# Trailing sums of the pooling moved to VectorE, a fifth first block, more last blocks by token halves, and the chain of 1/rms placed among them

## The chip, the cores and the metric

The kernel runs on one core of a Trainium2 chip, in one launch. The core has five engines with an instruction queue each: TensorE (PE: matmuls; the loads of its weights are listed as PEld), VectorE (DVE), ScalarE (ACT), GpSimd (POOL) and SyncE (SP, which here only starts transfers). The metric is the device time of one execution in microseconds (us). Lower is better.

## The reference

Two layers, each a token mixer and a feed-forward network (FFN) on 512 tokens of 1024 numbers, with a root-mean-square norm ahead of and behind each of the four parts. Cut to what the change touches:

```python
def rms_norm(x, w):
    return x * lax.rsqrt(jnp.mean(x * x, axis=-1, keepdims=True) + RMS_EPS) * w

def multiscale_pool(u, w_lin, scale):      # POOL_WINDOWS = (2, 4, 8, 16), 4 groups of 128
    cs = jnp.cumsum(groups, axis=1)
    for gi, win in enumerate(POOL_WINDOWS):
        pooled.append((c - prev) / cnt)    # trailing mean over win tokens
    mixed = jnp.stack(pooled, axis=2) - groups
    y = jnp.einsum('bsgc,gcd->bsgd', mixed, w_lin)
    return y * scale

def reference(x, ...):
    for l in range(DEPTH):                 # DEPTH = 2
        m = hybrid_mixer(rms_norm(x, mix_pre_norm[l]), ...)
        x = x + rms_norm(m, mix_post_norm[l])
        h = rms_norm(x, ffn_pre_norm[l])
        x = x + rms_norm(swiglu(h, ...), ffn_post_norm[l])
```

The mixer multiplies its input by one wide matrix whose columns feed a gated DeltaNet (q, k, v with a short convolution, two gates a and b), the pooling above, a retention and three gates; the three results go through a branch matrix each, are gated and added, and go through `w_out`. The FFN is `(silu(h @ w_gate) * (h @ w_up)) @ w_down` with 2816 hidden columns.

## The kernel before

**Layout.** The hidden dimension lies on the 128 partitions, in 8 tiles `k`; the 512 tokens lie along the free axis. A block is 128 output columns for all tokens: 8 products over `k` into one PSUM bank. Each product is three matmuls (`mm3`, L223 to L225), because weights and operands are split into a high and a low part: hh·wh, hl·wh, hh·wl. So a block is 24 matmuls of 128x512, or, if it is done by token halves, 48 of 128x256. The weights come by SyncE's queue into three buffers `raw`, and are split half a block at a time by ACT (`wh`, L233) and DVE (`wl`, L234) into `WB` = 8 buffers each.

**Order.** Generators are advanced by hand (`some(gen, n)`, `tasks`, `fill`) and so write the instructions in an order in which PE always has a next matmul; the splitting of weights runs ahead under a raised priority, and the scheduler of the framework then sets each engine's order. Engines execute in order and wait for each other by semaphores.

**Hand-over** (`hand_over`) is the passage from the mixer to the FFN and back; there are three inside the kernel, and a last one that writes the result. The last blocks of a stage (`LAST_OUT`, `LAST_DOWN` of them) are done by token halves h0 and h1. When a half is complete, `mean_square` sums its squares over the partitions with matmuls against ones (L268); DVE then takes 1/rms in eleven small operations in a chain (`rsv` L270, then L244 to L260, the last writes `rsy`), and `spread_new` copies it over the partitions with matmuls (L276). `step(h, ps, k)` then makes the new x of one tile k and half h: `pt` (L329) and `xt` (L330) on DVE, its high part `hh` (L229, ACT) and low part `hl` (L230, DVE), its square (ACT) and the running sum of squares (POOL, L290). The first blocks of the next stage do not wait for its own 1/rms: `group_step` multiplies three of them side by side (PSUM tiles `cx`), and the factor `rb` is applied to the results.

**Start of a mixer.** The first four blocks are the pooling's inputs. Behind `rb`, DVE writes them as `ku` (L1130); `pooled` makes the trailing sums `ft` by doubling, ten per layer, on POOL (L966); DVE then makes the mixed tile with one wide operation (L970) and two of 16 columns (L974, L977); and `pool_map` multiplies it on PE (L983), whose result ACT and DVE split into `oh` and `ol`. Among them stand the convolution of key block 0 (L608 to L629) and the two gates a, b of all heads: `abw` (L510, L511) is multiplied on PE (L516, 16 matmuls), the result scaled on DVE (`cv`, L519) and transposed on PE (L522).

## Time and profile before

| what | value |
|---|---|
| median of 3 runs | 1876.48 us (1874.4 to 1877.54) |
| profiled execution, its own time | 1876.93 us |
| its span in the trace | 1875.1 us |
| mean granted clock of TensorE | 0.989 of full speed |
| busy: PE, DVE, ACT, POOL | 1819.5, 1045.0, 711.9, 394.7 us |

The span is what the trace covers, from the first to the last recorded work; the profiled execution's time is 1.83 us more, and lies 0.45 us above the median. PE is busy for 97% of the span. [...]

### The profile page before, as it was taken

What the parts mean: (1) busy time and instruction counts of PE and PEld (TensorE: products, weight loads), DVE (VectorE), ACT (ScalarE), POOL (GpSimd) and SP (SyncE); (2) the same over time, 40 slices, a digit from 0 to 9 for tenths busy, and PEclk for the clock granted to TensorE, in tenths of its full rate; (3) what the DMA queues carried; (4) which work ended last, traced back from release to release, by engine and by line L of the source; (5) the groups of instructions that cost most, each with busy time, mean ns of one, the idle gap of its engine ahead of it and who ended that gap; (6) DMA issues with size and microseconds to landing.
All of it is one profiled execution on the core that took longest, in us unless ns stands there. A gap on an engine that the chain in (4) does not pass through costs nothing.

```text
span 1875.1 us, 24737 instructions
## 1 busy us (share of the span) xinstructions
PE 1819.5 (97%) x9286; PEld 1531.2 (82%) x9286; DVE 1045.0 (56%) x1973; ACT 711.9 (38%) x1259; POOL 394.7 (21%) x364
## 2 busy tenths in 40 slices
PE   8899999999999999999979999999999999999997
PEld 6677888888898888888867878888888888888887
DVE  7668667664438442344486786666644564324433
ACT  4553333343344333333345533334333443333332
POOL 4130211012223220222250302110121332102212
PEclk9899999999999999999989999999999999999998
DMA  5223212124225323223232222222243252333321
GB/s 194 70 80 93 74 60 71 60 87 146 91 71 188 96 96 102 92 100 95 76 118 93 80 83 62 69 72 67 90 135 101 70 188 92 102 93 98 101 90 46
DMA packets 65415, 177.70 MB, mean 95 GB/s; under 512 B 15376, under 2 KB 18448, under 8 KB 65296
## 3 DMA queue, kind: packets, MB, share of 16 engines
q1 hardware_dynamic: 54016, 172.78, 28.4%
q10 hardware_dynamic: 11280, 3.34, 0.8%
q8 instruction: 73, 1.20, 0.3%
q14 instruction: 46, 0.38, 0.1%
HBM read 167.18 MB, written 8.39 MB: 94 GB/s over the span
## 4 chain that ended last, share of the span: by engine, by line
PE 84%; DVE 9%; ACT 2%; issue 1%; POOL 1%; ACTq 1%; DMA 1%; SPq 0%; DVEq 0%; POOLq 0%
PE pp L223 24%; PE pp L225 24%; PE pp L224 24%; DVE ct L618 2%; DVE wl L234 2%; POOL ft L966 1%; DVE hl L230 1%; ACTq L787 1%; PE cx L820 1%; PE cx L913 1%; PE cx L903 1%; DVE xt L330 1%; PE cx L805 1%; PE fx L499 1%; ACT wh L233 1%
## 5 line engine op out<-in xcount | busy, mean ns | idle before, releaser
L233 ACT ACTIVATE wh<-raw 128x512 fp32r<-128x512 f32 x584 | 364.8, 629 | 718.4 <-PE pp L224 626.3
L223 PE MATMUL pp<-hh,wh 128*128 128x512 f32 x1568 | 623.7, 398 | 0.0
L225 PE MATMUL pp<-hh,wl 128*128 128x512 f32 x1568 | 614.1, 392 | 0.0
L224 PE MATMUL pp<-hl,wh 128*128 128x512 f32 x1568 | 612.5, 391 | 0.0
L234 DVE TENSOR_TENSOR wl<-raw,wh 128x512 fp32r<-128x512 f32 x584 | 418.0, 719 | 316.2 <-ACT wh L233 300.6
L225 PEld LDWEIGHTS pp<-hh,wl 128*128 128x128 f32 x1568 | 294.9, 188 | 63.9 <-issue 1.2
L223 PEld LDWEIGHTS pp<-hh,wh 128*128 128x128 f32 x1568 | 295.1, 188 | 61.2 <-issue 2.3
L224 PEld LDWEIGHTS pp<-hl,wh 128*128 128x128 f32 x1568 | 295.3, 188 | 59.4 <-issue 0.5
L223 PE MATMUL pp<-ah,wh 128*128 128x512 f32 (+1 forms) x418 | 149.1, 357 | 0.0
L225 PE MATMUL pp<-ah,wl 128*128 128x512 f32 (+1 forms) x418 | 148.6, 356 | 0.0
L224 PE MATMUL pp<-al,wh 128*128 128x512 f32 (+1 forms) x418 | 148.5, 355 | 0.0
L1255 POOL TENSOR_TENSOR gs<-gt,sg 128x512 f32<-128x512 f32 x44 | 56.7, 1288 | 314.3 <-ACT sg L1253 314.3
L1260 POOL TENSOR_TENSOR a<-gs,ut 128x512 f32<-128x512 f32 x44 | 70.2, 1594 | 136.1 <-DVE ut L1258 135.8
L290 POOL TENSOR_TENSOR sqa<-sqa,sq 128x256 f32<-128x256 f32 (+1 forms) x69 | 62.6, 907 | 127.9 <-ACT sq L283 108.6
L225 PEld LDWEIGHTS pp<-ah,wl 128*128 128x128 f32 x418 | 79.0, 189 | 11.3
L223 PEld LDWEIGHTS pp<-ah,wh 128*128 128x128 f32 x418 | 78.9, 189 | 11.3
L224 PEld LDWEIGHTS pp<-al,wh 128*128 128x128 f32 x418 | 79.0, 189 | 11.3
L234 DVE TENSOR_TENSOR al<-a,ah 128x512 fp32r<-128x512 f32 x44 | 31.3, 711 | 77.7 <-ACT ah L233 77.5
L1005 POOL TENSOR_TENSOR y<-y,ft 128x512 f32<-128x512 f32 x16 | 27.2, 1702 | 184.8 <-DVE ft L1004 95.3
L233 ACT ACTIVATE ah<-a 128x512 fp32r<-128x512 f32 x44 | 27.8, 632 | 89.2 <-POOL a L1260 89.2
L1258 DVE TENSOR_TENSOR ut<-pp,rb 128x512 f32<-128x512 f32 x42 | 29.0, 690 | 58.7 <-PE pp L225 58.7
L223 PE MATMUL pp<-yh,wh 128*128 128x256 f32 (+1 forms) x192 | 61.4, 320 | 0.0
(306 smaller groups left out, 2441.6 us busy)
## 6 DMA issues: line engine op xcount, KB each, us to landing
raw<-in_wi_dram SPq DMA_DIRECT2D x117, 512.0 KB
raw<-in_wgu_dram SPq DMA_DIRECT2D x88, 512.0 KB
raw<-in_wd_dram SPq DMA_DIRECT2D x44, 512.0 KB
raw<-in_wbr_dram SPq DMA_DIRECT2D x24, 512.0 KB
raw<-in_wo_dram SPq DMA_DIRECT2D x16, 512.0 KB
xd<-xt SPq DMA_DIRECT2D x24, 256.0 KB
xt<-xd SPq DMA_DIRECT2D x24, 256.0 KB
xt<-in_x_dram SPq DMA_DIRECT2D x16, 256.0 KB
```

What stands on the lines that cost most here:

```text
L223: T.matmul(ps, lhsT=w[0], rhs=m[0], start=start, stop=False)
L224: T.matmul(ps, lhsT=w[0], rhs=m[1], start=False, stop=False)
L225: T.matmul(ps, lhsT=w[1], rhs=m[0], start=False, stop=stop)
L230: V.scalar_tensor_tensor(out=lo, in0=src, scalar=scalar, in1=hi.bitcast(F32), op0=ALU.mult, op1=ALU.subtract)
L233: A.activation(out=hi, in_=src, func=AF.Copy)
L234: V.tensor_tensor(out=lo, in0=src, in1=hi.bitcast(F32), op=ALU.subtract)
L290: G.tensor_tensor(out=t, in0=acc[0], in1=acc[1], op=ALU.add)
L618: V.scalar_tensor_tensor(out=a2, in0=u[:, j : j + S], scalar=tap(j), in1=a, op0=ALU.mult, op1=ALU.add)
L1005: G.tensor_tensor(out=ys[n], in0=ys[n], in1=t, op=ALU.add)
L1255: G.tensor_tensor(out=gs, in0=gt, in1=sg, op=ALU.mult)
L1258: V.tensor_tensor(out=ut, in0=up, in1=rb, op=ALU.mult)
L1260: G.tensor_tensor(out=a, in0=gs, in1=ut, op=ALU.mult)
```

## The change

It moves the ten trailing sums of each layer from POOL to DVE (same tiles, same sizes; L966 becomes L975). A stage now starts with five blocks: three side by side, a fourth also by token halves (`alone`), and a fifth for all tokens (`last_block`); for the mixer the fifth is convolution block 0 of the keys, for the FFN the gate of column block 2, which were done a little later before. Six blocks of `w_out` and four of `w_down` go by token halves, rather than four and three; homes for the split weights of the last two weight tiles (`beside`) make room for them. The places of the steps and of the two chains of 1/rms change: all eight `step(0, …)` now stand among the last blocks of the old stage, the chain of h1 starts behind tile 4 of the h0 group, its `spread_new` stands before `alone(h0)`. In the mixer, key block 1 comes ahead of the first two pool maps, and the two products of the rotary tables with `rb` (`rotations`) are written later; on POOL they stand first all the same.

```diff
-LAST_OUT = 4
-LAST_DOWN = 3
+LAST_OUT = 6
+LAST_DOWN = 4
...
-        def __init__(self, src, cut=False):
+        def __init__(self, src, cut=False, home=None):
+            self.home = home or (lambda a: wpool.tile([P, S], F32R, tag=a, bufs=WB, name=nm(a)))
...
-                wh = wpool.tile([P, S], F32R, tag="wh", bufs=WB, name=nm("wh"))
-                wl = wpool.tile([P, S], F32R, tag="wl", bufs=WB, name=nm("wl"))
+                wh, wl = self.home("wh"), self.home("wl")
...
         r = mean_square(accs[0])
-        some(p1, 4)
+        with tc.issue_after(nc.cur_bb.bb.instructions[-1]):
+            some(p1, 5)
         ps0 = spread_new(r)
...
-        for k in range(3):
+        for k in range(KT):
             step(0, ps0, k)
             some(p1, 2)
         rest(p1)
-        step(0, ps0, 3)
         ws, pss = [weights(src) for src in srcs[:3]], [psum_c() for _ in range(3)]
+        w4th, ps4 = weights(srcs[3]), psum_p()
+
+        def alone(sl):
+            for k in range(KT):
+                group_step([w4th], [ps4], hs, sl, k)
+                yield
+
         for k in range(KT):
             group_step(ws, pss, hs, h0, k)
-            if k == 0:
+            if k == 4:
                 r = mean_square(accs[1])
-            if k == 4:
-                ps1 = spread_new(r)
-            if k < 4:
-                step(0, ps0, k + 4)
-            elif k >= 5:
-                step(1, ps1, k - 5)
+        f = alone(h0)
+        ps1 = spread_new(r)
+        for k in range(3):
+            step(1, ps1, k)
+            some(f, 3)
+        r = mean_square(pre[0])
         for k in range(KT):
             group_step(ws, pss, hs, h1, k)
-            if k == 1:
-                r = mean_square(pre[0])
-            if k == 4:
-                A.activation(out=rb[:, h0], in_=spread_new(r), func=AF.Copy)
             if k + 3 < KT:
                 step(1, ps1, k + 3)
-        f = fourth_block(srcs[3], hs, pss)
+            if k == 6:
+                A.activation(out=rb[:, h0], in_=spread_new(r), func=AF.Copy)
+        rest(alone(h1))
+        f = last_block(srcs[4], hs, pss)
+        pss.append(ps4)
...
-        return vec[:, l, V_PRE1 : V_PRE1 + KT], [wi[l, B_PU + g] for g in range(4)]
+        return vec[:, l, V_PRE1 : V_PRE1 + KT], [wi[l, B_PU + g] for g in range(4)] + [wi[l, B_K]]
...
-        return vec[:, l, V_PRE2 : V_PRE2 + KT], [wgu[l, 0, 0], wgu[l, 0, 1], wgu[l, 1, 0], wgu[l, 1, 1]]
+        return vec[:, l, V_PRE2 : V_PRE2 + KT], [wgu[l, f // 2, f % 2] for f in range(5)]
...
                 t = ft()
-                G.tensor_tensor(out=t[:, first:], in0=src[:, first:], in1=src[:, first - d : S + pad - d], op=ALU.add)
+                V.tensor_tensor(out=t[:, first:], in0=src[:, first:], in1=src[:, first - d : S + pad - d], op=ALU.add)
...
-            G.tensor_tensor(out=t, in0=t, in1=rb, op=ALU.mult)
+
+        def rotations():
+            for t in (crb, srb):
+                G.tensor_tensor(out=t, in0=t, in1=rb, op=ALU.mult)
+            yield
...
-        tasks = convs("k", 0) + [pool_map(0), pool_map(1)] + convs("k", 1)
+        tasks = convs("k", 0) + convs("k", 1) + [pool_map(0), pool_map(1)]
...
-        tasks += convs("v", 0) + p(7)
+        tasks += [rotations()] + convs("v", 0) + p(7)
...
-                    held[n] = weights(wo[l, n])
+                    held[n] = weights(wo[l, n], home=beside() if n >= KT - 2 else None)
...
-                            held[i // 8] = weights(wd[l, half, i // 8])
+                            last = half == 1 and i // 8 >= KT * HALF // 8 - 2
+                            held[i // 8] = weights(wd[l, half, i // 8], home=beside if last else None)
```

The first of three places is VectorE's queue at the start of the first mixer, up to `cv`, the scaled gates a and b. The names: `ft` are trailing sums, or in L608 and L616 the convolution's input; `kr`, `qr`, `vc`, `mask` are the four mixed tiles of the pooling, `pc` their first 16 columns; `wl` are low parts of weights, `ct` steps of the convolution. Before:

```order
L234 TENSOR_TENSOR wl_702<-raw_682,wh_701 128x512 [waits PE_49,Activation_49]
L974 TENSOR_TENSOR pc_388<-ft_384,kc 128x16 [waits DVE_49]
L977 TENSOR_TENSOR vc_386<-pc_388,ku_349 128x16 [waits DVE_49]
L970 SCALAR_TENSOR_TENSOR mask_399<-ft_397,ku_349 128x496 [waits Pool_49]
L974 TENSOR_TENSOR pc_401<-ft_397,kc 128x16 [waits DVE_49]
L608 TENSOR_TENSOR ft_444<-pp_411,rb_127 128x512 [waits PE_49]
L977 TENSOR_TENSOR mask_399<-pc_401,ku_349 128x16 [waits DVE_49]
L234 TENSOR_TENSOR wl_736<-raw_732,wh_735 128x512 [waits DMAHW2_49,Activation_49]
L618 SCALAR_TENSOR_TENSOR ct_449<-ft_444,vec,ct_447 128x512 [waits Activation_49]
L618 SCALAR_TENSOR_TENSOR ct_451<-ft_444,vec,ct_449 128x512 [waits DVE_49]
L618 SCALAR_TENSOR_TENSOR ct_453<-ft_444,vec,ct_451 128x512 [waits DVE_49]
L519 TENSOR_TENSOR cv_482<-fx_459,rb_127 16x512 [waits PE_49]
```

and after:

```order
L979 SCALAR_TENSOR_TENSOR vc_419<-ft_417,ku_384 128x496 [waits DVE_49]
L983 TENSOR_TENSOR pc_421<-ft_417,kc 128x16
L975 TENSOR_TENSOR ft_426<-ft_424 128x525 [waits DVE_49]
L986 TENSOR_TENSOR vc_419<-pc_421,ku_384 128x16 [waits DVE_49]
L234 TENSOR_TENSOR wl_700<-raw_680,wh_699 128x512 [waits PE_49,Activation_49]
L975 TENSOR_TENSOR ft_428<-ft_426 128x521 [waits DVE_49]
L234 TENSOR_TENSOR wl_734<-raw_730,wh_733 128x512 [waits DMAHW2_49,PE_49,Activation_49]
L975 TENSOR_TENSOR ft_430<-ft_428 128x513 [waits DVE_49]
L616 TENSOR_TENSOR ft_442<-pp_341,rb_127 128x512
L979 SCALAR_TENSOR_TENSOR mask_432<-ft_430,ku_384 128x496 [waits DVE_49]
L983 TENSOR_TENSOR pc_434<-ft_430,kc 128x16
L527 TENSOR_TENSOR cv_524<-fx_486,rb_127 16x512 [waits PE_49]
```

The sums, which POOL did beside this queue, now stand in it one by one, and `cv` has moved ahead of the convolution's three steps.

The second place is TensorE's queue a little further on in the same mixer: the end of the 16 matmuls of the gates (`abw`), the transposes of `cv`, and the first pool map (`sw` holds the map's weights). Before:

```order
L516 MATMUL fx_459<-hh_125,abw_348 128x512
L516 MATMUL fx_459<-hl_126,abw_348 128x512
L983 MATMUL fx_476<-kr_366,sw_351 128x512 [waits DMAHW4_49,DVE_49,Activation_49]
L223 MATMUL pp_510<-hh_111,wh_511 128x512
L224 MATMUL pp_510<-hl_112,wh_511 128x512
L225 MATMUL pp_510<-hh_111,wl_512 128x512
L522 MATMUL fx_484<-kc,cv_482 128x8 [waits DVE_49]
L522 MATMUL fx_484<-kc,cv_482 128x8 x3
L223 MATMUL pp_510<-hh_113,wh_511 128x512
```

and after:

```order
L524 MATMUL fx_486<-hh_125,abw_383 128x512
L524 MATMUL fx_486<-hl_126,abw_383 128x512
L223 MATMUL pp_459<-hh_123,wh_476 128x512
L224 MATMUL pp_459<-hl_124,wh_476 128x512
L225 MATMUL pp_459<-hh_123,wl_477 128x512
L223 MATMUL pp_459<-hh_125,wh_476 128x512
L224 MATMUL pp_459<-hl_126,wh_476 128x512
L225 MATMUL pp_459<-hh_125,wl_477 128x512
L530 MATMUL fx_526<-kc,cv_524 128x8 [waits DVE_49,Activation_49]
L530 MATMUL fx_526<-kc,cv_524 128x8 x3
L992 MATMUL fx_531<-kr_399,sw_386 128x512 [waits DMAHW4_49,PE_49]
L223 MATMUL pp_578<-hh_111,wh_579 128x512
```

The pool map of `kr` has moved behind the transposes, and 6 matmuls rather than 3 stand between the gates' last matmul and the transposes. What no row here shows: key block 1, 24 matmuls of the fifth block's kind, begins ahead of the gates rather than behind them.

The third place is VectorE's queue in the hand-over from the first mixer to its FFN, at the chain of 1/rms of the half h1 (`rsv` to `rsy`, 128x2 each). Before:

```order
L329 TENSOR_TENSOR pt_5229<-m_4884,fx_4991 128x256
L250 TENSOR_TENSOR rsb_5163<-rsa_5161,rsv_5155 128x2 [waits DVE_49]
L230 SCALAR_TENSOR_TENSOR hl_5005<-xt_4073,vec,hh_5004 128x256 [waits Activation_49]
L252 SCALAR_TENSOR_TENSOR rsa_5165<-rsb_5163 128x2 [waits DVE_49]
L230 SCALAR_TENSOR_TENSOR hl_5007<-xt_4076,vec,hh_5006 128x256 [waits Activation_49]
L254 SCALAR_TENSOR_TENSOR rsy_5167<-rsa_5165,rsy_5159 128x2 [waits DVE_49]
L330 SCALAR_TENSOR_TENSOR xt_4076<-pt_5229,vec,xt_4076 128x256
L256 SCALAR_TENSOR_TENSOR rsa_5169<-rsy_5167 128x2 [waits DVE_49]
L234 TENSOR_TENSOR wl_5462<-raw_5459,wh_5461 128x512 [waits DMAHW0_49]
L258 TENSOR_TENSOR rsb_5171<-rsa_5169,rsv_5155 128x2 [waits DVE_49]
L230 SCALAR_TENSOR_TENSOR hl_5009<-xt_4076,vec,hh_5008 128x256 [waits Activation_49]
L260 SCALAR_TENSOR_TENSOR rsy_5173<-rsb_5171,rsy_5167 128x2 [waits DVE_49]
```

and after:

```order
L234 TENSOR_TENSOR wl_5379<-raw_5221,wh_5378 128x512 [waits PE_49,Activation_49]
L270 TENSOR_SCALAR rsv_5298<-fx_5293 128x2 [waits PE_49]
L244 TENSOR_SCALAR rsi_5300<-rsv_5298 128x2 [waits DVE_49]
L246 TENSOR_SCALAR rsy_5302<-rsi_5300 128x2 [waits DVE_49]
L248 TENSOR_TENSOR rsa_5304<-rsy_5302 128x2 [waits DVE_49]
L250 TENSOR_TENSOR rsb_5306<-rsa_5304,rsv_5298 128x2 [waits DVE_49]
L252 SCALAR_TENSOR_TENSOR rsa_5308<-rsb_5306 128x2 [waits DVE_49]
L254 SCALAR_TENSOR_TENSOR rsy_5310<-rsa_5308,rsy_5302 128x2 [waits DVE_49]
L256 SCALAR_TENSOR_TENSOR rsa_5312<-rsy_5310 128x2 [waits DVE_49]
L258 TENSOR_TENSOR rsb_5314<-rsa_5312,rsv_5298 128x2 [waits DVE_49]
L260 SCALAR_TENSOR_TENSOR rsy_5316<-rsb_5314,rsy_5310 128x2 [waits DVE_49]
L329 TENSOR_TENSOR pt_5348<-m_4601,fx_5345 128x256 [waits PE_49]
```

Before, steps of the half h0 (`xt`, `pt`, `hl`) and a low part of weights stand between the links of the chain; now the links follow each other, and the first step of the half h1 comes behind the last.

## Rows read from the trace of the kernel before

**Rows 1.** TensorE's waits over the span: for what, us in total, times, longest

```profile
PE fx L276 <- DVE rsy L260: 10.7, 8, 2.5
PE fx L522 <- DVE cv L519: 9.4, 1, 9.4
PE fx L516 <- DVE qr L977: 8.5, 1, 8.5
```

**Rows 2.** Windows (us, busy PE, PEld, DVE, ACT, POOL, granted clock): both mixers' starts

```profile
46.00:55.00 9.00, 0.18 (x1) 0.00 (x0) 7.57 (x14) 0.75 (x2) 4.20 (x5) 0.65 0.21 58
971.00:984.00 13.00, 4.52 (x11) 3.47 (x11) 11.96 (x18) 0.91 (x2) 11.01 (x11) 0.61 0.00 0
```

**Rows 3.** TensorE's timeline at the starts: start, us, instruction, count, idle before

```profile
40.83 0.39 PE L516 MATMUL fx<-hh,abw 128*128 128x512 f32 x1
...
44.45 1.02 PE L983 MATMUL fx<-kr,sw 128*128 128x512 f32 x2
...
55.54 1.87 PE L522 MATMUL fx<-kc,cv 16*128 16x8 f32 x8 [9.36 <-DVE cv L519]
57.34 0.80 PE L223 MATMUL pp<-hh,wh 128*128 128x512 f32 x1
...
62.50 1.02 PE L983 MATMUL fx<-qr,sw 128*128 128x512 f32 x2
...
979.67 0.77 PE L516 MATMUL fx<-hh,abw 128*128 128x512 f32 x1 [8.48 <-DVE qr L977]
...
985.40 1.02 PE L983 MATMUL fx<-kr,sw 128*128 128x512 f32 x2
...
987.27 1.05 PE L522 MATMUL fx<-kc,cv 16*128 16x8 f32 x8
```

**Rows 4.** VectorE's timeline at the starts of both mixers

```profile
34.82 1.89 DVE L1130 TENSOR_TENSOR ku<-cx,rb 128x512 f32<-128x512 f32 x3 [1.77 <-ACT rb L381]
...
38.47 1.52 DVE L970 SCALAR_TENSOR_TENSOR kr<-ft,ku 128x496 f32<-128x496 f32 x1 [1.17 <-POOL ft L966]
...
50.36 0.68 DVE L970 SCALAR_TENSOR_TENSOR mask<-ft,ku 128x496 f32<-128x496 f32 x1 [1.16 <-POOL ft L607]
50.95 0.17 DVE L974 TENSOR_TENSOR pc<-ft,kc 128x16 f32<-128x16 f32 x1
...
54.81 0.67 DVE L519 TENSOR_TENSOR cv<-fx,rb 16x512 f32<-16x512 f32 x1
...
965.26 1.88 DVE L1130 TENSOR_TENSOR ku<-cx,rb 128x512 f32<-128x512 f32 x3 [0.82 <-ACT rb L455]
```

**Rows 5.** GpSimd's timeline at the first mixer's start: first and last trailing sums

```profile
37.38 2.09 POOL L966 TENSOR_TENSOR ft<-ku 128x527 f32<-128x527 f32 x2
...
46.04 4.28 POOL L966 TENSOR_TENSOR ft<-ft 128x525 f32<-128x525 f32 x3
```

**Rows 6.** Windows as in rows 2: in the first hand-over, around the second

```profile
569.00:575.00 6.00, 5.02 (x30) 5.05 (x31) 5.74 (x16) 2.81 (x8) 1.44 (x2) 0.72 0.54 188
920.00:965.00 45.00, 42.05 (x314) 39.24 (x314) 39.09 (x106) 22.27 (x52) 13.02 (x16) 1.00 0.40 133
```

**Rows 7.** Timeline of the first hand-over, and TensorE's last L276 of the kernel

```profile
563.73 0.14 DVE L270 TENSOR_SCALAR rsv<-fx 128x2 f32<-128x2 f32 x1
563.77 0.28 PE L223 MATMUL cx<-hh,wh 128*128 128x256 f32 x1
...
564.97 0.28 PE L224 MATMUL cx<-hl,wh 128*128 128x256 f32 x1
...
569.98 0.68 PE L276 MATMUL fx<-kc,rsy 128*128 128x128 f32 x4 [2.46 <-DVE rsy L260]
570.70 0.42 DVE L329 TENSOR_TENSOR pt<-m,fx 128x256 f32<-128x256 f32 x1 [0.26 <-PE fx L276]
...
584.27 0.87 DVE L230 SCALAR_TENSOR_TENSOR hl<-xt,vec,hh 128x256 fp32r<-128x256 f32 x2
...
1865.78 0.55 PE L276 MATMUL fx<-kc,rsy 128*128 128x128 f32 x1 [2.12 <-DVE rsy L260]
```

More of the change, by code (lines that the diff above doesn't have):

```diff
@@ L351, in rest, with last_block @@
             pass
-    def fourth_block(src, hs, res):
+    def last_block(src, hs, res):
         ps = psum_p()
@@ L376, in begin @@
             group_step(ws, pss, hs, WHOLE, k)
-        f = fourth_block(srcs[3], hs, pss)
+        f = last_block(srcs[3], hs, pss)
         some(f, 1)
@@ L382, in begin @@
         rest(f)
+        rest(last_block(srcs[4], hs, pss))
         return x_in, hs, rb, pss
@@ L408, in hand_over @@
                     send(h0, k // 2)
-                some(p1, 1)
+                some(p1, 2)
             rest(p1)
@@ L430, in hand_over @@
         rest(p1)
-        step(0, ps0, 3)
         ws, pss = [weights(src) for src in srcs[:3]], [psum_c() for _ in range(3)]
+        w4th, ps4 = weights(srcs[3]), psum_p()
[3 more added lines that the diff above has]
+                yield
         for k in range(KT):
             group_step(ws, pss, hs, h0, k)
-            if k == 0:
+            if k == 4:
                 r = mean_square(accs[1])
-            if k == 4:
-                ps1 = spread_new(r)
-            if k < 4:
-                step(0, ps0, k + 4)
-            elif k >= 5:
-                step(1, ps1, k - 5)
+        f = alone(h0)
[4 more added lines that the diff above has]
+        r = mean_square(pre[0])
         for k in range(KT):
             group_step(ws, pss, hs, h1, k)
-            if k == 1:
-                r = mean_square(pre[0])
-            if k == 4:
-                A.activation(out=rb[:, h0], in_=spread_new(r), func=AF.Copy)
             if k + 3 < KT:
                 step(1, ps1, k + 3)
-        f = fourth_block(srcs[3], hs, pss)
+            if k == 6:
[3 more added lines that the diff above has]
+        pss.append(ps4)
         some(f, 1)
@@ L636, in conv_one @@
         def conv_one(b, ch, key):
-            res = []
-            yield from project(wi[l, b], hs, res)
+            res = firsts[4:] if key == ("k", 0) else []
+            if not res:
+                yield from project(wi[l, b], hs, res)
             o = conv(res[0], ch, key)
@@ L1204, in mixer, with beside, home @@
             ms, acc, held = [], None, {}
+            def beside():
+                t = {a: keep.tile([P, D], F32R, tag="wq", bufs=H, name=nm(a)) for a in ("wh", "wl")}
+                n = dict(wh=0, wl=0)
+                def home(a):
+                    n[a] += 1
+                    return t[a][:, (n[a] - 1) * S : n[a] * S]
+                return home
             def out_block(n, sl, res):
                 if n not in held:
-                    held[n] = weights(wo[l, n])
+                    held[n] = weights(wo[l, n], home=beside() if n >= KT - 2 else None)
                     ms.append(keep.tile([P, S], F32, tag="y", bufs=KT, name=nm("m")))
@@ L1236, in run @@
             def run(f, i):
-                if 2 * f + i < 4:
+                if 2 * f + i < len(firsts):
                     return firsts[2 * f + i]
@@ L1266, in ffn, with beside @@
                 held = {}
+                free = iter(("gt", "sg", "gt", "sg", "gs", "ut", "gs", "ut"))
+                def beside(a):
+                    return tl(next(free), 2, dt=F32R)
                 def down(n, sl, res):
```

## The prediction

> **What bounds the kernel now.** TensorE is busy for 97% of the span, so I looked first for where it is not: its list of waits [rows 1]. Three entries stand out, and the change touches all three. One wait of 9.4 us at the transposes of `cv` (L522) and one of 8.5 us at the gates' matmuls (L516) are the starts of the two mixers; 10.7 us in eight pieces are waits of `spread_new` (L276) for the end of the chain of 1/rms, 2.1 us of them at the very end of the kernel [rows 7], which the change hardly touches. So 8.6 us lie in the three hand-overs inside the kernel.
>
> Then the windows: around the long waits the granted clock is a mix, 0.65 and 0.61 [rows 2], so each wait costs more than its length. The timeline prices that. [...] Start of the first mixer: 9.36 idle, 12 × 0.204 = 2.4 for the matmuls, and 0.8 because the transposes took 1.87 rather than 1.05 us: **12.6 us lost**. Start of the second: 8.48 idle, and the 16 matmuls behind it took 979.67 to 985.40, 5.73 rather than 3.62 us: **10.6 us lost**. In the first hand-over the longest L276 wait, 2.46 us [rows 7], is followed by a stretch of six microseconds at 0.72 [rows 6]: 0.28 of 6 us missing, halving the speed for some 3.4 us, costs about 1.5 us. I take the same for the third hand-over, of the same shape. The second has no wait so long, and its window shows 1.00 [rows 6]. Hand-overs: 8.6 + 3.0 = **11.6 us lost**.
>
> What VectorE waits for at the starts is GpSimd: "[1.17 <-POOL ft L966]" [rows 4]. The ten sums there ran from 37.38 to 50.32, 12.9 us [rows 5]. And while they run, VectorE itself is slow: the same wide operation L970 took 1.52 us beside them and 0.68 us behind them [rows 4].
>
> **Sums on VectorE.** The trace shows none. The nearest row is `ku`, a two-input operation of 128x512: three took 1.89 us, 0.60 each with a tail [rows 4]; 527 columns make 0.62. From below: not under 0.60. From above: 1.45, the distance by which the 1.52 us operations would follow each other. I take 0.62, since after the change GpSimd holds only the two rotary products in this stretch.
>
> [...]
>
> **First mixer.** Along the new order VectorE has, from 34.82 [rows 4]: four `ku` 2.4, ten sums 6.2, four wide mixing operations at 0.6 (0.68 less the overlap) 2.4, seven of 16 columns at 0.09 (50.95, next at 51.04) 0.6, three `wl` and the convolution's input at 0.6 2.4. That is 48.9, and `cv` takes 0.67: 49.6. TensorE stood at 40.83 at the gates [rows 3]; now 18 matmuls of key block 1 come first (44.9), then the gates (48.5), then 6 more (49.9). So `cv` is just ready and the 9.36 us are gone, with the low clock. `cv` also stood behind three convolution steps at 0.6 to 0.8 and no longer does; these come later, where the next to need them is many matmuls away. What becomes late next: the four pool maps, closer together now, each needing ScalarE's `oh` and VectorE's `ol` (0.7 us each by the width of `cv`) and one of two PSUM banks. I put 2.0 us for that (bounds 0 and 6): **−10.6**.
>
> **Second mixer.** From 965.26: `ku` 2.4, eight sums 5.0, three wide 1.8, six narrow 0.5 and the cast: the gates' operand at 975.2. TensorE came there at 971.19 (979.67 less 8.48) and has 22 matmuls more first: 976.2. No wait. The gates end at 979.8, `cv` at 980.9 (VectorE is free at 979.6), TensorE is there at 980.7. Behind it the new order crowds all four maps into some twenty instructions: 0.9 for the first `oh` (a map of 0.46, then 0.7), 0.4 and 0.5 for banks, 0.5 for an `ol`: with 0.2 at `cv` 2.5 us (bounds 0 and 7): **−8.1**.
>
> **Hand-overs.** Before, the chain of h1 took from 563.73 to 569.98 [rows 7], since steps stand between its links; TensorE had 24 matmuls meanwhile, and 128x256 go at 0.120 us (563.77 to 564.97 for ten), 2.9 us. After, the links follow each other: eleven operations of 0.15 to 0.2, 2.2 us with the wait for L268's result some 2.5, and 27 matmuls (3.2 us) to cover it. That holds if the eight steps of h0 are done by then: 24 operations at 0.35 to 0.40 and three `wl` are 11 us, beside 17 us of TensorE (102 matmuls of the last blocks and five tiles of h0). The h1 steps with the next chain were 14.4 us of VectorE (570.70 to 585.14); from L276 to the last `hl` TensorE has some 14 us (102 matmuls of 128x256, two L276, one L268). So that is even, and I leave 1.7 us of waits in each hand-over (bounds 0 and the present 3.9): 11.6 − 5.1 = **−6.5**. Moving a wait's start alone would bring nothing; what shortens it is the interleaved work taken out of the chain.
>
> **Halves.** 48 × 0.120 less 24 × 0.226 is 0.33 us per block. Two more blocks of `w_out` in two layers 1.3; one of `w_down` (33 products) in two layers 0.9; the fourth block in three hand-overs 1.0: **+3.1** (no cover: TensorE pays). The fifth block replaces one done later: 0. `beside` adds no instruction: 0, unless the fourth weight tile comes late (below).
>
> **Sum.** 1876.93 (the profiled execution, span 1875.1, 0.45 above the median) − 10.6 − 8.1 − 6.5 + 3.1 = **1854.8, so 1855**.
>
> **Rivals.**
> *A, the wait moves to the pool maps.* For it: all four maps within twenty instructions in the second mixer, two banks. Against: each wait is under a microsecond by the rows. At the upper bounds, 4 and 4.5 us more: 1863.5.
> *B, hand-overs give nothing.* The chain of h1 stands behind both `wl` of the fourth block's weights; there are three `raw` buffers, so this tile is fetched only after an earlier one is split. If it comes as TensorE reaches L276, the wait stays. Against: some 4 us of VectorE's work and over 10 of TensorE's lie between. 1876.9 − 18.7 + 3.1 = 1861.3.
> *C, all clean.* Half a microsecond left at each of the five places: 34.8 less 2.5, 1876.9 − 32.3 + 3.1 = 1847.7.
> *D, VectorE stays as slow as it is beside GpSimd now; slower.* If the sums and mixing operations take 1.45 and the narrow ones 1.0 us, `cv` comes 14 × 0.84 + 7 × 0.9 = 18 us later at each start; the waits stay, with the low clock behind (3.2 and 2.1): 18 + 3 − 1 each, 1854.8 + 39 = 1894. It decides (ends above 1880.2) from some 12.7 us per start, 0.75 us on each wide operation. Against: two rotary products of GpSimd cannot cover twenty operations.
> *E, no effect.* The order shows the sums in VectorE's queue, so only gains and losses that cancel make it: sums and mixing operations at about 1.25 us.
>
> **Chances.** Forecast 0.52, A 0.14, B 0.16, C 0.12, D 0.03, E 0.03. The range runs from just under C to just over A, 1846 to 1866, and holds some 0.85. A difference of 0.2% (3.75 us) is about what a measurement of this kernel can tell from none: faster 0.94, same 0.03, slower 0.03.
>
> **What would show it.** Right: no wait over 1.5 us at L530 and L524; granted clock 1.0 from 36 to 75 us and behind the second `ku`; L975 near 0.7 us, L979 0.68 and L983 0.17; waits at L276 together under 6 us, and no low clock in the hand-overs. Wrong: L975 at 1 us or more (D, E), waits at L992 or at products of `oh` over 3 us (A), an L276 wait over 2 us behind `wl` (B). The whole fails if another place, quiet now, loses what these win, above all VectorE's later backlog of convolution steps.

## The result, and the profile after

| | before | after |
|---|---|---|
| median | 1876.38 us (4 runs) | 1849.58 us (4 runs, 1848.3 to 1850.55) |
| ratio to before | | 0.9857, 95% interval 0.9844 to 0.9870 |
| profiled execution, span | 1876.93, 1875.1 us | 1850.22, 1848.4 us |
| mean granted clock | 0.989 | 0.996 |

The forecast was 1855, with a range of 1846 to 1866; the kernel became 26.8 us faster, 5 us more than forecast. TensorE's list of waits over the span (for what, us in total, times, longest), where [rows 1] stood before:

```profile
PE cx L223 <- ACT wh L233: 6.1, 1, 6.1
PE fx L276 <- DVE rsy L260: 4.0, 4, 2.1
PE fx L507 <- DVE cv L633: 3.2, 8, 0.6
PE cx L224 <- DVE hl L230: 2.7, 4, 1.8
PE cx L912 <- ACT c L914: 2.5, 1, 2.5
```

The waits of 9.4 and 8.5 us are gone (the 6.1 us at the head of the list are the kernel's very first matmul), and those at L276 fell from 10.7 to 4.0 us, 2.1 of them at the end of the kernel. The window over the first mixer's start, then two stretches in the second mixer which are told of below (columns as in [rows 2]):

```profile
36.00:75.00 39.00, 39.00 (x176) 30.65 (x175) 34.91 (x78) 20.55 (x32) 3.17 (x8) 1.00 0.21 71
970.00:973.00 3.00, 2.58 (x4) 1.44 (x5) 2.06 (x5) 1.00 (x3) 0.00 (x0) 0.59 0.55 180
1107.00:1113.00 6.00, 3.93 (x16) 3.35 (x17) 2.49 (x4) 4.13 (x8) 2.13 (x3) 0.79 0.28 90
```

TensorE is busy for all 39 us of the first, at full clock (1.00). VectorE's timeline there, the answer to [rows 4]:

```profile
37.37 1.39 DVE L975 TENSOR_TENSOR ft<-ku 128x527 f32<-128x527 f32 x2
38.68 0.66 DVE L979 SCALAR_TENSOR_TENSOR kr<-ft,ku 128x496 f32<-128x496 f32 x1
39.26 0.16 DVE L983 TENSOR_TENSOR pc<-ft,kc 128x16 f32<-128x16 f32 x1
39.35 0.69 DVE L975 TENSOR_TENSOR ft<-ft 128x525 f32<-128x525 f32 x1
39.96 0.17 DVE L986 TENSOR_TENSOR kr<-pc,ku 128x16 f32<-128x16 f32 x1
...
48.93 0.67 DVE L527 TENSOR_TENSOR cv<-fx,rb 16x512 f32<-16x512 f32 x1
```

A sum takes 0.69 us and the next operation starts 0.61 us after it; the first two, one behind the other, took 1.39. The mixing operation takes 0.66, not 1.52 us, the narrow ones 0.16, not 1.03. TensorE's timeline at the transposes shows no idle time before them:

```profile
49.81 0.39 PE L225 MATMUL pp<-hh,wl 128*128 128x512 f32 x1
50.13 1.05 PE L530 MATMUL fx<-kc,cv 16*128 16x8 f32 x8
51.11 1.13 PE L992 MATMUL fx<-kr,sw 128*128 128x512 f32 x2
```

The start of the second mixer, TensorE's timeline from the gates' transposes on:

```profile
967.56 1.03 PE L530 MATMUL fx<-kc,cv 16*128 16x8 f32 x8
968.52 1.12 PE L992 MATMUL fx<-kr,sw 128*128 128x512 f32 x2
970.42 0.72 PE L223 MATMUL pp<-oh,wh 128*128 128x512 f32 x1 [0.78 <-ACT oh L229]
970.94 1.91 PE L992 MATMUL fx<-qr,sw 128*128 128x512 f32 x2
972.64 1.68 PE L992 MATMUL fx<-vc,sw 128*128 128x512 f32 x2
973.57 0.98 PE L224 MATMUL pp<-ol,wh 128*128 128x512 f32 x1
```

Two pool maps take 1.91 and 1.68 rather than 1.02 us: behind a wait of 0.78 us the granted clock was lower (0.59 over these 3 us, above). The first hand-over, chain of h1 and its L276, then L276 of the next chain and one late `hl`, VectorE first, then TensorE, as in [rows 7]:

```profile
555.76 0.16 DVE L270 TENSOR_SCALAR rsv<-fx 128x2 f32<-128x2 f32 x1 [0.98 <-PE fx L268]
...
557.54 0.16 DVE L260 SCALAR_TENSOR_TENSOR rsy<-rsb,rsy 128x2 f32<-128x2 f32 x1
```

```profile
558.90 0.60 PE L276 MATMUL fx<-kc,rsy 128*128 128x128 f32 x4
...
569.35 0.68 PE L276 MATMUL fx<-kc,rsy 128*128 128x128 f32 x4 [0.62 <-DVE rsy L260]
573.07 0.38 PE L224 MATMUL cx<-hl,wh 128*128 128x256 f32 x1 [0.30 <-DVE hl L230]
```

The chain took 1.94 us from first to last link, where before 6.25 us passed from its first link to L276 [rows 7], and was ready 1.2 us ahead of TensorE. What is left is 0.62 and 0.30 us.

To see where the time went, I cut the spans at the same places of the program: the first L276 that makes `rb`; the first transpose of the convolved values (L499 before, L507 after); the first product of `w_out`; the first of each half of `w_down`; the last L276 that makes `rb` of the second mixer; the end of the last transfer's issue, some 3 us ahead of the end of the span. Kernels with the fifth block have 20 matmuls of 0.227 us (4.5 us) in hand-over 2 that else stand in the start of mixer 2: the 24 of the fifth block, less four, because the last L276 comes behind 22 matmuls of its block before and behind 18 after. So the sum of these two stages is a line of its own. In us, from the profiles of all kernels with the sums on either engine (a2 is the changed kernel once more; e1 to e4 are told below):

```
stage             before   after      a2      e1      e2      e3      e4
to first L276       33.1    33.2    32.9    33.0    33.3    35.6    33.5
mixer 1 start      150.8   138.6   138.6   150.9   138.6   138.3   148.0
mixer 1 rest       329.5   330.6   330.8   330.4   329.3   333.1   329.5
hand-over 1        177.4   173.7   173.7   173.7   177.3   177.3   173.7
FFN 1              179.5   179.5   179.5   179.5   179.5   179.5   179.5
hand-over 2         93.9    95.4    95.4    95.4    93.9    94.0    95.4
mixer 2 start      147.7   135.3   133.7   141.7   138.8   138.2   141.8
mixer 2 rest       329.8   333.2   333.4   330.3   330.1   330.4   329.2
hand-over 3        177.4   173.7   173.7   173.7   176.1   176.1   173.7
FFN 2              179.5   179.5   179.5   179.5   179.5   179.5   179.5
end                 73.4    72.8    73.3    73.3    72.9    72.9    72.8
h-o 2 + m 2 st.    241.6   230.7   229.1   237.1   232.7   232.2   237.2
all               1872.0  1845.5  1844.4  1861.3  1849.4  1855.0  1856.6
```

Before to after: mixer 1 start −12.2; hand-overs −3.7, −3.0 (+1.5 less the 4.5 moved in) and −3.7; mixer 2 start −7.9 (−12.4 with the 4.5 moved out); the end −0.7; and two stages grew, the rests of the mixers by 1.2 and 3.4. Together −26.5.

### The profile page after: what moved, and what is told of

Read it like the earlier page. It is cut to its first block, busy times and chain, and to the rows that moved or that the text cites. A ratio compares the mean times of both kernels' runs of the same rounds, so it can differ in the third digit from the quotient of the medians.

```text
span 1848.4 us, 25207 instructions
## 1 busy us (share of the span) xinstructions
PE 1816.2 (98%) x9520; PEld 1537.0 (83%) x9520; DVE 1045.4 (57%) x1995; ACT 710.9 (38%) x1270; POOL 376.1 (20%) x350
## 4 chain that ended last, share of the span: by engine, by line
PE 88%; DVE 7%; ACT 2%; issue 1%; ACTq 1%; DMA 0%; POOL 0%; SPq 0%; DVEq 0%; POOLq 0%
PE pp L223 25%; PE pp L225 25%; PE pp L224 25%; DVE ct L626 2%; DVE wl L234 1%; PE cx L829 1%; PE cx L224 1%; PE cx L922 1%; PE cx L912 1%; PE cx L225 1%; PE cx L223 1%; PE fx L268 1%; PE cx L814 1%; PE fx L507 1%; DVE hl L230 1%
## 5 line engine op out<-in xcount | busy, mean ns | idle before, releaser
L223 PE MATMUL pp<-hh,wh 128*128 128x512 f32 (+1 forms) x1592 | 627.8, 394 | 0.0
L225 PE MATMUL pp<-hh,wl 128*128 128x512 f32 (+1 forms) x1592 | 617.9, 388 | 0.0
L224 PE MATMUL pp<-hl,wh 128*128 128x512 f32 (+1 forms) x1592 | 616.7, 387 | 0.0
L223 PE MATMUL pp<-ah,wh 128*128 128x512 f32 (+1 forms) x376 | 134.7, 358 | 0.0
L225 PE MATMUL pp<-ah,wl 128*128 128x512 f32 (+1 forms) x376 | 134.4, 357 | 0.0
L224 PE MATMUL pp<-al,wh 128*128 128x512 f32 (+1 forms) x376 | 134.4, 357 | 0.0
L225 PEld LDWEIGHTS pp<-ah,wl 128*128 128x128 f32 x376 | 71.0, 189 | 10.3
L224 PEld LDWEIGHTS pp<-al,wh 128*128 128x128 f32 x376 | 71.0, 189 | 10.3
L225 PE MATMUL pp<-yh,wl 128*128 128x256 f32 (+1 forms) x224 | 66.8, 298 | 0.0
L224 PE MATMUL pp<-yl,wh 128*128 128x256 f32 (+1 forms) x224 | 66.8, 298 | 0.0
```

What stands on the lines that cost most here:

```text
L223: T.matmul(ps, lhsT=w[0], rhs=m[0], start=start, stop=False)
L224: T.matmul(ps, lhsT=w[0], rhs=m[1], start=False, stop=False)
L225: T.matmul(ps, lhsT=w[1], rhs=m[0], start=False, stop=stop)
```

## The experiments

**Which part does what.** Theory: the sums on GpSimd, with VectorE slow beside them, are the loss at the starts, and the new hand-over is a second, separate gain. Rival: the new order and the cover of the fifth block bring the gain at the starts, whichever engine sums. Four kernels, timed together beside before (1876.61).

e1, the changed kernel with one letter back:

```diff
-                V.tensor_tensor(out=t[:, first:], in0=src[:, first:], ...
+                G.tensor_tensor(out=t[:, first:], in0=src[:, first:], ...
```

> The changed kernel with the ten trailing sums of each layer put back on GpSimd, all else as changed. Theory (the sums on GpSimd, with VectorE slow beside them, are the chain at the mixers' starts): cv comes at about 55 us in the first mixer, where TensorE waits for it from 49.9, so a wait of 5 us with the low clock behind it, 8 us lost; in the second a wait of 3 us for the gates' operand and some at cv, 7 us lost: 1849.6 + 15, about 1865. Rival (the new order and the fifth block's cover alone bring the gain at the starts, whichever engine sums): within 2 us of 1849.6.

1866.91 us, 0.9948 of before (0.9933 to 0.9963). The rival falls. TensorE's waits in 33 to 75 us, and in 962 to 1000 us, of e1:

```profile
PE fx L530 <- DVE cv L527: 8.8, 1, 8.8
...
PE fx L524 <- DVE qr L986: 6.8, 1, 6.8
```

Both waits of before are back, larger than I expected at `cv`, since its place in VectorE's queue went behind the convolution. With the sums on GpSimd the new order of tasks is even a loss: e4, without it, has mixer 1's start 2.9 us shorter.

e2, the kernel before with the same letter changed:

```diff
-                G.tensor_tensor(out=t[:, first:], in0=src[:, first:], ...
+                V.tensor_tensor(out=t[:, first:], in0=src[:, first:], ...
```

> The kernel before with the ten sums on VectorE and nothing else changed. Theory: at 0.61 us a sum cv is ready at 45.6 us in the first mixer, as TensorE comes to L522, so 11 to 12 us are won; in the second the gates' operand is ready at 975.2 where TensorE comes at 971.2, so 4 us of the wait stay with some low clock and 4 to 5 us are won: about 1861. Rival (the order and the cover are what counts): within 3 us of 1876.4.

1855.19 us, 0.9885 (0.9870 to 0.9899): **21.4 us from this edit alone**, more than the theory gave. Mixer 1's start is as short as after the whole change (138.6). VectorE, then TensorE at the same place in e2:

```profile
45.24 0.67 DVE L519 TENSOR_TENSOR cv<-fx,rb 16x512 f32<-16x512 f32 x1
```

```profile
44.61 1.02 PE L983 MATMUL fx<-kr,sw 128*128 128x512 f32 x2
...
46.26 1.05 PE L522 MATMUL fx<-kc,cv 16*128 16x8 f32 x8
```

`cv` is there with TensorE, as worked out (45.6 expected, 45.91 its end). In the second mixer the wait at the gates is 0.8 us, not the 4 expected: TensorE came there 12.0 us behind L276 rather than 7.0, because the scheduler had put 54 rather than 32 matmuls ahead of the gates, as many as in the changed kernel. The gates' operand was ready 12.6 us behind L276, later than the 11.0 expected, since the first two sums ran beside GpSimd's rotary products there (954.78 to 957.80) and took twice as long as in the first mixer:

```profile
955.39 2.97 DVE L966 TENSOR_TENSOR ft<-ku 128x527 f32<-128x527 f32 x2
```

e3, the kernel before with the sums on VectorE and the new tasks, and e4, the changed kernel without these two:

```diff
-        tasks = convs("k", 0) + [pool_map(0), pool_map(1)] + convs("k", 1)
+        tasks = convs("k", 0) + convs("k", 1) + [pool_map(0), pool_map(1)]
...
-        tasks += convs("v", 0) + p(7)
+        tasks += [rotations()] + convs("v", 0) + p(7)
```

> The kernel before with the sums on VectorE and the changed order of the mixer's tasks, but with the old hand-over, four first blocks and four and three last blocks by halves. What it lacks against the changed kernel is the hand-over's worth. Theory of the prediction (hand-overs bring 6.5 us less 3.1 for the halves): 3.4 us above the changed kernel, 1853. Theory from comparing the two traces (each of the three hand-overs 3.7 to 4.0 us shorter, the end 0.9): 12 us above it, about 1862.

> The changed kernel with the sums on GpSimd and the old order of the mixer's tasks: the new hand-over, the five first blocks and the six and four last blocks by halves are what is left of the change. If the parts add up, the hand-overs bring 12 us and the fifth block covers some 4 us more of the second mixer's wait: 1860 to 1864. If, as the prediction has it, they bring 3.4 net: 1869 to 1873.

e3: 1854.22 us, 0.9886 (0.9871 to 0.9901), 1 us from e2: the new task order is worth nothing measurable, since e2 has the same cover at the gates already. Its profiled execution was its slowest (1859.62) and spends 3.8 us more than e2 in mixer 1's rest, of which more below. e4: 1862.94 us, 0.9929 (0.9913 to 0.9946): the hand-over with its blocks is worth 13.7 us by itself, 3.7 in each of hand-overs 1 and 3. The two gains are 21.4 and 13.7 us apart, 26.8 together: they do not add up. By the stages, the hand-overs keep theirs, but e4 also shortens the start of mixer 1 by 2.8 us, which nothing is left of once the sums are on VectorE; hand-over 2 with mixer 2's start gains only 2.0 us over e2; and the rests of the mixers lose.

**What in the hand-over does it.** The parts: new places of steps and chains; a fifth block, whose fourth half-wise block (`alone`) covers VectorE; more last blocks by halves. Theory as predicted: the extra halves hide the h0 steps.

e5, the changed kernel:

```diff
-LAST_OUT = 6
-LAST_DOWN = 4
+LAST_OUT = 4
+LAST_DOWN = 3
```

> The changed kernel with four and three last blocks by halves, as before, rather than six and four. Theory (the extra halves are what hides the eight h0 steps): TensorE reaches the first group some 6 us earlier, 11.8 rather than 17.6 us after its first L276, while VectorE needs 11 to 12 us for the steps, so the chain of h1 starts late and each hand-over loses 1 to 2 us, less 0.6 for the halves saved: 1851 to 1854. Rival (the new places alone do it, the extra halves only cost): 1849.6 less 2.2, 1847.4.

1844.09 us, 0.9827 (0.9813 to 0.9840), faster than the changed kernel. Hand-overs 0.8, 0.4 and 0.8 us shorter: the rival holds, the extra halves only cost. e8, old places with the fifth block and the extra halves:

```diff
-        for k in range(KT):
+        for k in range(3):
             step(0, ps0, k)
             some(p1, 2)
         rest(p1)
+        step(0, ps0, 3)
...
-            if k == 4:
+            if k == 0:
                 r = mean_square(accs[1])
-        f = alone(h0)
-        ps1 = spread_new(r)
-        for k in range(3):
-            step(1, ps1, k)
-            some(f, 3)
+            if k == 4:
+                ps1 = spread_new(r)
+            if k < 4:
+                step(0, ps0, k + 4)
+            elif k >= 5:
+                step(1, ps1, k - 5)
+        rest(alone(h0))
```

> The changed kernel with steps and chains of the hand-over at their old places in the program (chain of h1 behind tile 0, its spread at tile 4, four of the h0 steps inside the group), but with five first blocks and six and four last blocks by halves. Theory (the places bring the gain): each hand-over 3.7 us longer again, 1849.6 + 11, about 1861. Rival (the cover of the extra halves brings it): hand-overs stay near 174 us, 1850 to 1852.

1851.64 us, 0.9871 (0.9857 to 0.9884). Between the two: hand-overs 174.5, 97.1 and 176.5, so 0.8 to 2.8 us longer than after, not 3.7. Its waits in 545 to 585 us:

```profile
PE fx L276 <- DVE rsy L260: 1.3, 1, 1.3
PE fx L268 <- ACT sq L283: 0.8, 1, 0.8
```

The scheduler did not interleave the chain of h1 here either (3.3 us from its first link to its last, 552.50 to 555.82); with the steps moved later, the last square comes late for L268. e10, e5 without the fifth block and `alone`, with lists of four first blocks as before:

```diff
-        w4th, ps4 = weights(srcs[3]), psum_p()
...
-        f = alone(h0)
         ps1 = spread_new(r)
         for k in range(3):
             step(1, ps1, k)
-            some(f, 3)
...
-        rest(alone(h1))
-        f = last_block(srcs[4], hs, pss)
-        pss.append(ps4)
+        f = last_block(srcs[3], hs, pss)
```

> The kernel e5_last_4_3 without the fifth block: four first blocks again, the fourth for all tokens at the end, the chains and steps at their new places. Theory (the 24 matmuls of the fourth block's h0 half are the cover under which VectorE makes the first h1 steps): TensorE reaches the h1 group 2.9 us earlier and waits at hl there, each hand-over 3 to 5 us longer, 1844 + 9 to 15, less 1 for the halves, and some more at the gates of the second mixer: 1853 to 1860. Rival (the new place of the chain alone is the gain): 1843 to 1846.

1849.35 us, 0.9853 (0.9840 to 0.9867). In hand-over 1 the steps are now: before 177.4, new places alone (e10) 174.9, with the fifth block (e5) 172.9, with the extra halves (after) 173.7. So in this order the places give 2.5 us, the fifth block 2.0 (0.3 of cost already taken off), and the extra halves take 0.8 away. The other order, e8, splits the gain differently: with the old places and all the cover hand-over 1 is only 0.8 us longer than after. So the parts overlap, and no share belongs to one of them alone. TensorE in e10, 545 to 585 us, waits where the cover is missing, at the first operands of h1:

```profile
PE cx L223 <- ACT hh L229: 1.0, 1, 1.0
PE cx L224 <- DVE hl L230: 0.6, 2, 0.3
```

These waits are 0.6 us more than the 0.9 that are left in e5. The rest of the 2.0 us is the clock behind the wait of 1.0 us: it fell in hand-over 1 of e10, but not in its hand-over 2, where the same wait stands (columns as in [rows 2]):

```profile
561.00:567.00 6.00, 5.64 (x32) 5.59 (x33) 6.00 (x20) 2.95 (x8) 2.56 (x3) 0.72 0.47 175
932.00:938.00 6.00, 5.73 (x41) 5.36 (x42) 6.00 (x19) 3.54 (x10) 2.58 (x3) 1.00 0.47 175
```

0.28 of six us are 1.7 us. In hand-over 2 with mixer 2's start e5 and e10 differ by 0.2 us only.

**What was lost in the mixers.** e7, the changed kernel with the first two maps ahead of key block 1, and e6, with the rotary products taking no unit of the tasks' order:

```diff
-        tasks = convs("k", 0) + convs("k", 1) + [pool_map(0), pool_map(1)]
+        tasks = convs("k", 0) + [pool_map(0), pool_map(1)] + convs("k", 1)
```

```diff
         def rotations():
             for t in (crb, srb):
                 G.tensor_tensor(out=t, in0=t, in1=rb, op=ALU.mult)
-            yield
+            yield from ()
```

> The changed kernel with the first two pool maps ahead of key block 1 again, as before. Theory from the first four runs (with the sums on VectorE the new task order is worth nothing, and in the second mixer it crowds the four maps, which costs 2 us): about 1848. Rival (key block 1 ahead is needed as cover for the gates): a wait of 1 to 4 us at the gates or at cv in each mixer, 1852 to 1858.

> The changed kernel with the rotary products taking no unit in the order of the mixer's tasks. In the profile after, the second mixer's later part is 3.4 us longer than before, most of it one wait of 2.5 us for ScalarE with the low clock behind it. If the shift by one unit makes this: 330 rather than 333 us there, and about 1846.5. If it is a thing of single executions: within 1 us of 1849.6, and the wait appears in one profile and not in another whatever the order.

e7: 1844.07 us, 0.9830 (0.9817 to 0.9844). e6: 1844.43 us, 0.9831 (0.9818 to 0.9845). Stages of the second set:

```
stage              after      e5      e6      e7      e8     e10      b1      b2
to first L276       33.2    33.4    33.0    33.1    33.3    33.5    33.2    33.4
mixer 1 start      138.6   138.7   138.6   138.3   138.6   138.4   138.3   138.3
mixer 1 rest       330.6   330.7   330.3   330.7   330.7   331.5   330.7   330.7
hand-over 1        173.7   172.9   173.7   173.7   174.5   174.9   172.9   173.6
FFN 1              179.5   179.5   179.5   179.5   179.5   179.5   179.5   179.5
hand-over 2         95.4    95.0    95.4    95.4    97.1    91.1    95.0    95.8
mixer 2 start      135.3   133.6   133.6   132.4   133.6   137.7   131.9   132.1
mixer 2 rest       333.2   330.4   329.6   330.4   330.4   330.7   332.4   330.5
hand-over 3        173.7   172.9   173.7   173.7   176.5   174.9   172.9   173.6
FFN 2              179.5   179.5   179.5   179.5   179.5   179.5   179.5   179.5
end                 72.8    72.9    72.8    72.8    72.8    72.9    72.9    73.0
h-o 2 + m 2 st.    230.7   228.6   229.0   227.8   230.6   228.8   226.9   227.8
all               1845.5  1839.5  1839.8  1839.5  1846.4  1844.7  1839.3  1839.9
```

e7 has mixer 2's start 2.9 us shorter: with two maps earlier, no wait there. But e6 has it 1.7 shorter as well, with the same instructions from the start of hand-over 2 up to that place and the same wait of 0.78 us. The window over the two maps in e6:

```profile
970.00:973.00 3.00, 3.00 (x10) 1.83 (x11) 2.90 (x6) 2.05 (x4) 0.00 (x0) 1.00 0.54 180
```

Full clock, where the changed kernel's profile showed 0.59. So I ran the changed kernel again, and the two faster edits together (b1: e5 and e7; b2: the same with three and two last blocks by halves).

> The changed kernel itself once more, on the chip of the next three. Three kernels of the second four are each 5 us faster than it, and in their profiles the second mixer has no low clock at its pool maps (971 to 974 us after) and none behind the wait for ScalarE (1110 us after), though the instructions up to the first of these places are the same in e6_rot_no_unit. If both stretches belong to this kernel: 1849.6 within 1 us, and both at the lower level again. If they belong to single executions: 1845, or a profile without them.

> The changed kernel with four and three last blocks by halves and the first two pool maps ahead of key block 1: the two edits that were faster, together. If each keeps its own share (halves 2.0 us in the hand-overs, the order 2.9 us at the second mixer's start, the missing low clock counted once): 1842. If they only did the same thing twice: 1844.

> As b1_4_3_maps_first, with three and two last blocks by halves. Cover theory: with four and three TensorE had 11.8 us for the 11 us of the h0 steps, just enough; now it has 3 us less, some 9, so each of three hand-overs waits 2 us and may see the low clock behind it, less 0.3 saved: 1847 to 1851. Rival (the cover was not needed at all): 1 us faster than b1.

a2: 1847.92 us (1846.42 to 1849.15), 0.9842 (0.9829 to 0.9856). The pool maps ran at full clock this time (1.00 over 970.33 to 973.33), 133.7 us for mixer 2's start, so the low clock there belongs to single executions; the long rest of mixer 2 (333.4) is there again. b1: 1844.07 us, 0.9822 (0.9809 to 0.9835), no better than either edit alone: hand-overs 172.9 as in e5, mixer 2's start 131.9 (e7: 132.4), but a rest of 332.4. b2: 1844.83 us, 0.9827 (0.9814 to 0.9841); hand-overs 0.7 us longer than b1's in spite of fewer halves, so the cover begins to be missed only here, and by 1 us, not 2.

The long rest: ScalarE's timeline in the changed kernel ahead of the wait of 2.5 us at L912:

```profile
1095.42 11.30 ACTq L796 DMA_DIRECT2D uc<-c  x16
1106.77 1.67 ACT L233 ACTIVATE wh<-raw 128x512 fp32r<-128x512 f32 x3 [11.06 <-DMA uc<-c]
1108.35 0.58 ACT L914 ACTIVATE c<-cx 128x512 f32<-128x512 f32 x1
```

ScalarE issues 16 small transfers one behind the other, 0.71 us each, then three weight splits that queued up, and only then the `c` that TensorE waits for; behind the wait the clock falls (0.79 over 1107 to 1113). The traces of all kernels separate two causes. Here are when TensorE comes to this place (L903 before, L912 after; us from the first transpose of the convolved values), how long the 16 issues take, and how long TensorE waits for whom:

```
kernel, mixer   TensorE there   16 issues   wait, for
before, 1            21.5          10.5     0.9  ScalarE
before, 2            21.6          11.1     1.5  ScalarE
e6, 1                21.6          11.3     1.7  ScalarE
e6, 2                21.6          10.5     0.9  ScalarE
after, 1             20.2          10.5     1.7  GpSimd
after, 2             20.2          11.3     2.5  ScalarE
a2, 2                20.2          11.5     2.7  ScalarE
e5, 2                20.2          10.5     1.7  GpSimd
```

The first cause is the task order. Where the rotary products are a unit of their own (all kernels but before, e2, e4 and e6), 98 rather than 104 matmuls stand ahead of this place, TensorE is there 1.4 us earlier, and waits 0.8 us longer, in both mixers. e6 takes this unit out, and its rest of mixer 2 is 329.6 us, as expected if the shift by one unit makes it. The second cause is the issues: where they take 11.1 to 11.5 us, the wait is 0.6 to 1.0 us longer again, and that happens in one mixer and not in the other of the same kernel (in b1 they begin 0.3 us later instead). The clock fell behind the waits of 2.0 to 2.7 us here in after (0.72 over 1109 to 1115), a2 and b1 (0.72 over six us each), and e3 (in e3 it is the first mixer, a wait of 2.6 us, the 3.8 us above). It did not fall behind one of 2.5 us in e10's first mixer, whose rest is 0.8 us longer than e5's, as the wait is (331.5 and 330.7; 2.5 and 1.7), and behind none of 1.7 us (in after's first mixer 1.00 over 195 to 201). Why the issues take longer in one mixer than in another was not tested.

## Why the prediction was right, and where it was off

**Sums: right.** 0.62 forecast, 0.61 from start to start. The bound of 1.45 (rivals D and E) does not apply, and e1 shows the other side of it: GpSimd's sums, and what VectorE loses beside them, cost 17 us in the changed kernel. The rotary products of GpSimd can do it too: beside them two sums took 2.97 us in e2, where the changed kernel has 1.39.

**First mixer: right.** The forecast's 0.226 us for a matmul of 128x512, and the 0.204 it added for each of the 12 behind the old wait, are from [rows 3]: the 16 of the gates took 40.83 to 44.45, 0.226 us each, and those 12 took 57.34 to 62.50, 0.43 us each. `cv` was forecast to start at 48.9 and started at 48.93; TensorE at 49.9, and it began L530 at 50.13. The 2.0 us left for the pool maps were not needed: −12.2, not −10.6.

**Second mixer: right in kind.** TensorE reached the gates 11.8 us after L276 (951.10 to 962.91; forecast 12.0) without a wait, and the wait came where forecast, at the first `oh` (0.78 against 0.9). −8.1 forecast; −7.9 in the profile with the low clock, −9.5 in the one without. Rival A, the wait moving to the maps, happened at this size and not at 7 us.

**Hand-overs: the term that was mis-sized.** −6.5 and +3.1 for the halves, −3.4 in sum, were forecast; the stages measured −3.7, −3.0, −3.7 and −0.7 at the end, −11.1. The halves were priced right: e5 saves 2.0 us in the hand-overs, 1.8 forecast for those it takes back there. So the gain without them was some 14 us, not 6.5 (of the end's part little is the change's: e2, with the old end, has 72.9 us too).

By the forecast's own terms the first and the third hand-over come to −2.7 each (3.9 us of waits down to 1.7, 1.5 of low clock gone, 1.0 paid for halves). There the mechanism held: the listed waits fell from 4.0 to 0.9 us, and the low clock, 1.7 us, is gone (in hand-over 1 of after 1.00 over 556 to 575). Only what stays was put too high, 1.7 for 0.9.

The second hand-over is where the forecast failed, with +1.6 (0.9 of waits up to 1.7, and 0.8 paid for halves) for a measured −3.0. Leaving 1.7 us "in each hand-over" made it longer, since no more than 0.9 us of L276 stood there. And I counted only L276 as loss, "8.6 us lie in the three hand-overs"; in the second one the profile lists 1.9 us for others, twice what it lists for L276. TensorE's waits there before, 920 to 965 us, then in the same stage after:

```profile
PE fx L268 <- ACT sq L283: 1.2, 1, 1.2
PE fx L276 <- DVE rsy L260: 0.9, 1, 0.9
PE cx L224 <- DVE hl L230: 0.5, 2, 0.3
PE cx L223 <- ACT hh L229: 0.2, 1, 0.2
```

```profile
PE fx L276 <- DVE rsy L260: 0.6, 1, 0.6
PE cx L224 <- DVE hl L230: 0.3, 1, 0.3
```

That is 2.8 us before and 0.9 after. And as much again lies in gaps too short for the list: all of them taken together, listed or not, a 128x256 matmul in hand-over 2 had 0.134 us until the next start before (45.97 us for 342, summed over the timeline) and 0.125 after (56.80 for 456), where 0.120 is the undisturbed distance; 0.0098 on some 400 matmuls is 3.9 us, twice what the listed waits give (2.8 less 0.9).

The reason given for the gain, that the interleaved work is taken out of the chain, is seen in the trace (1.94 us), but it is not the whole of it: added to the places, the cover of `alone` gave hand-over 1 another 2.0 us, most of it low clock (e10, e5), and with the old places the chain of h1 was free of other work as well (e8). The forecast also had 17 us of TensorE, extra halves included, beside the 11 us of steps; so much was not needed. In e5, with four and three, TensorE comes to L276 16.4 us behind the first L276 (541.97 to 558.41), and the chain is ready at 557.26. Rival B did not happen: VectorE waited 0.98 us for L268, not for the weights.

**What the sum left out:** the rests of the mixers, 1.2 and 3.4 us longer, put at nothing. "VectorE's later backlog", named as the danger, is not the cause there: the unit of the rotary products brings TensorE to L912 1.4 us earlier, ahead of GpSimd in the first mixer and of ScalarE's queue of transfers in the second, where the low clock (0.72 over 1109 to 1115) adds 1.7 us.

**A faster version:** e5, e6, e7 and b1 lie at 1844.1 to 1844.4 us, 32.5 us faster than before; e5 is the simplest, the change without its extra halves. They do not gain by the same thing: e5 saves 2.0 us in the hand-overs, e6 the earlier arrival at L912, e7 1.2 us at the start of mixer 2, and the profiles of all three are free of the two stretches of low clock (1.7 us each) in the second mixer of after. b1 has the gains of e5 and e7 in its stages and loses 2 us of them in a rest with low clock. e5 and e6 together were not run.

## What to carry to other kernels

When two engines that share a stretch are slow side by side, look at both rows: the operation that waits for GpSimd, and the one that is twice as long beside it (here 1.52 against 0.66 us). Moving ten operations per layer to the engine that looked fuller made it no busier (1045.0 and 1045.4 us), because its twelve mixing operations fell from 10.9 to 3.9 us in sum (first mixer), and the ten sums took 7.0. And price a hand-over by the distance of the matmuls in it, not by the list of waits alone; then take each edit back by itself, since one of those that came with the gain only cost.

## What the runs showed of the hardware

- VectorE's wide operations overlap in the rows of after: a sum's row has 0.69 to 0.70 us, and the next operation starts 0.61 us after it (39.35, then 39.96); the distance between two is what counts in a queue. The same wide operation took 1.52 us with sums on GpSimd beside it (before, [rows 4]) and 0.66 without (after). How GpSimd slows it, no run shows.
- The same wait of 0.78 us, with the same instructions ahead of it, was followed by the lower clock in one profile of the changed kernel (after, 0.59 over three us) and not in another (a2, 1.00), nor in e6 (1.00), nor in e5, whose start of mixer 2 is as short as e6's (133.6 us). A wait of 2.4 to 2.5 us had it behind it in hand-overs 1 and 3 of before (0.72 over 569 to 575 and over 1499 to 1505), but in e2 only in the first of these (0.72 over six us; 1.00 behind the third's). One stretch of it cost 1.7 us (0.28 of six), and whether a wait brought it differed from one execution to the next.
- A transfer issued from ScalarE's queue held it for 0.65 to 0.72 us, sixteen of them for 10.5 to 11.5 us, with its next operations behind them.
